# The feed-forward of a hybrid decoder layer in parts of 6, 14, 12 and 12 gated blocks, where it was 8, 16, 8 and 12

## The chip, the cores and the metric

The kernel runs on one core of a Trainium2 chip. The metric is the device time of one launch in microseconds. Before the change three runs took 1701.47, 1701.69 and 1701.87 us; the median is 1701.69.

## What is computed

One layer of a decoder trunk, for a prompt of 256 positions and a sample group of 8 × 4 positions that share the weights; 288 positions in all, model width 2048, feed-forward width 5632. Cut to what matters here:

```
z  = x @ w_in                        -> h, Bg, Cg, q, k, v, g_a, g_b
x1 = LN1(ALPHA*x + (sigmoid(g_a)*(A @ w_a) + sigmoid(g_b)*(B @ w_b)) @ w_out)
a, b = split(x1 @ w_up, 2)           # 5632 columns each
a    = causal width-3 depthwise convolution of a
y  = LN2(ALPHA*x1 + (silu(a) * b) @ w_down)
```

A is a gated short convolution and B an attention over dilated windows. The caches and convolution states that go with them are returned too.

## The kernel before

All activations lie transposed: 128 features on the partitions, the 288 positions along the free dimension, stored as two halves of 144. A weight block is 128 output columns by all its input rows, loaded as 16 (or fewer) tiles of 128 × 128. Everything is float32; to multiply at full rate each operand is split into a rounded high part and the rest (`split`, L263: a cast on ACT, a subtraction on DVE), and a product adds three matmuls per tile: high × high (L257), low × high (L258), high × low (L259).

`product` (L237 and on) multiplies one block. It takes the weights that were split one call ago and has the next block loaded: `prepare` gets a buffer `wst` (three of them), has SP issue the load (L205), for every third or fourth block has SP issue a copy of a cache page from memory to memory (L161, `out_o_rest`), and splits the block into pairs `whi`/`wlo` of up to eight tiles each (four pairs). The result goes to one of five accumulators `acc`.

The feed-forward is the part from line 1202 on. Its 44 gated blocks are made in parts, whose sizes stand in `THIRDS`. In each part:

- for each gated block an up product for a (48 matmuls), then ACT brings it into `u`, the convolution runs on ACT and DVE (`cy`), a second up product for b, DVE gates (`ya`), and the split into `yah`/`yal` (ACT, DVE);
- then 16 down products, one for each block of 128 output features, each with 3 matmuls for each gated block of the part; DVE adds their result to the residual `dd` (L1259 in part 0, L1261 later).

The layout of `w_down` in memory follows the parts: a down block of part 0 is 8 tiles, 512 KB.

Part 0 differs. It starts before LN1's deviation is known: its up products multiply `x_gb`, the values ahead of the norm with two more columns (290 instead of 288), and `normed` (L1195 to L1198) applies mean and deviation to the result afterwards. Between the gated blocks of this part the residual `dd` itself is normed, a share of its 16 blocks after each gated block: POOL multiplies and adds (L1241, L1242), ACT scales (L1243). While part 0's down products run, `dd` is split into `xh`/`xl`, the input of the later parts. Part 1 also carries a step of the second norm's factors with each gated block.

The order of instructions on each engine is made by a scheduler when the kernel is built; it interleaves products where it expects a wait. Each engine then runs its list strictly in that order.

Of the kernel before, what the change touches and what calls it, by code (L numbers as in the profile page):

```python
# [30 lines left out]
FF = 5632  # L31
KF = FF // P
HK = KD // 2
THIRDS = (8, 16, 8, 12)
NG, NH = 3, 4
DIL = (1, 4, 16)
BAND = 128
# [70 lines left out]
def layer_kernel(ctx: ExitStack, tc: tile.TileContext, ins, outs):  # L108
# [14 lines left out]
    def sb(pl, shape, tag, dt=F32, bufs=None):  # L123
        return pl.tile(shape, dt, tag=tag, name=nm(tag), bufs=bufs)
# [49 lines left out]
    def weight_list():  # L174
# [8 lines left out]
        f = wd = 0  # L183
        for nf in THIRDS:
            for _ in range(2 * nf):
# [1023 lines left out]
    sums = []  # L1209
    for part, nf in enumerate(THIRDS):  # L1210
        gh = sb(big, [P, KD, T], "yah", F32R)
# [133 lines left out]
def _lay_out(i):  # L1345
# [17 lines left out]
    wd, k0 = [], 0  # L1363
    for nf in THIRDS:
        w = a["w_down"][k0 * P : (k0 + nf) * P].reshape(nf, P, KD, P)
# [98 lines left out]
```

## Time and profile before

| | |
|---|---|
| median of three runs | 1701.69 us |
| the profiled execution: time, span | 1701.91 us, 1700.1 us |
| part 0: up products, down products | 909.44 to 1004.16, 1004.16 to 1051.20 us |
| part 1 (16 blocks) | 1051.20 to 1333.44 us |
| part 2 (8 blocks) | 1333.44 to 1474.56 us |
| part 3 (12 blocks) and the last norm | from 1474.56 us |
| mean granted TensorE clock | 0.999 |

The span runs from the first to the last instruction of the core. The borders of the parts are the starts of their first matmuls. In a row of a timeline stand the start, the duration, the engine, the line, the operation, the tile written and those read, the shape and the count; in brackets how long the engine was idle ahead of it and what ended that.

### The profile page before, as it was taken

The page shows a single profiled execution, that of the slowest core. Times are in us where ns is not written, and L with a number is a line of the kernel's source. Part 1 is how long each engine was busy: PE and PEld are TensorE (multiplying, and loading weights), DVE is VectorE, ACT ScalarE, POOL GpSimd, SP SyncE. Part 2 cuts the span into 40 slices and gives each one's busy share as a digit, 9 for nine tenths or more (in the row PEclk, how much of TensorE's full clock was granted, in tenths as well). Part 3 has the DMA queues.
Part 4 walks back from the last instruction along what each step waited for, and adds up shares of the span by engine and source line. Part 5 has one row for each costly group of instructions (what it writes and reads, how often), then busy time and mean ns, then how long its engine had stood idle before and what let it go on. Part 6 is the DMA issues. An engine that isn't in the chain of part 4 may idle for free.

```text
span 1700.1 us, 34305 instructions
## 1 busy us (share of the span) xinstructions
PE 1692.8 (100%) x14094; PEld 1689.6 (99%) x14094; DVE 1197.0 (70%) x1548; ACT 943.0 (55%) x1684; POOL 398.3 (23%) x528
## 2 busy tenths in 40 slices
PE   9999999999999999999999999999999999999998
PEld 9999999999999999999999999999999999999998
DVE  5476779889887776655888886776554555555576
ACT  6477686665666655544546664555433454444455
POOL 0123242223332121111454440111100010011175
PEclk9999999999999999999999999999999999999999
DMA  8778777666678988577766658666666667766553
GB/s 314 273 295 350 285 282 312 245 251 245 248 290 313 333 308 335 214 261 255 280 237 223 226 214 322 225 257 225 230 238 225 223 227 249 293 223 250 200 175 112
DMA packets 61532, 436.16 MB, mean 257 GB/s; under 512 B 7936, under 2 KB 12032, under 8 KB 23680
## 3 DMA queue, kind: packets, MB, share of 16 engines
q1 hardware_dynamic: 60080, 430.15, 68.7%
q10 hardware_dynamic: 1296, 3.83, 0.6%
q8 instruction: 110, 1.80, 0.4%
q14 instruction: 46, 0.38, 0.1%
HBM read 427.50 MB, written 94.53 MB: 307 GB/s over the span
## 4 chain that ended last, share of the span: by engine, by line
PE 99%; ACT 0%; DMA 0%; SPq 0%; DVE 0%; ACTq 0%; issue 0%
PE acc L257 32%; PE acc L258 32%; PE acc L259 32%; PE acc L342 1%; ACT yah L1148 0%; DMA yah<-in_x 0%; PE acc L443 0%; PE att L490 0%; PE acc L490 0%; SPq L297 0%; ACT xh L309 0%; PE acc L1129 0%; PE acc L1125 0%; PE long L490 0%; PE acc L1126 0%; ACT yal L309 0%
## 5 line engine op out<-in xcount | busy, mean ns | idle before, releaser
L263 DVE TENSOR_TENSOR wlo<-wst,whi 128x1024 fp32r<-128x1024 f32 (+1 forms) x579 | 743.9, 1287 | 392.5 <-ACT whi L263 390.1
L263 ACT CAST whi<-wst 128x1024 fp32r<-128x1024 f32 (+1 forms) x579 | 588.6, 1019 | 652.8 <-PE acc L258 588.8
L257 PE MATMUL acc<-xh,whi 128*128 128x288 f32 (+1 forms) x3216 | 920.3, 286 | 0.0
L258 PE MATMUL acc<-xl,whi 128*128 128x288 f32 (+1 forms) x3216 | 920.0, 286 | 0.0
L259 PE MATMUL acc<-xh,wlo 128*128 128x288 f32 (+1 forms) x3216 | 920.0, 286 | 0.0
L257 PEld LDWEIGHTS acc<-xh,whi 128*128 128x128 f32 x3216 | 607.8, 189 | 0.5 <-issue 0.4
L258 PEld LDWEIGHTS acc<-xl,whi 128*128 128x128 f32 x3216 | 607.8, 189 | 0.0
L259 PEld LDWEIGHTS acc<-xh,wlo 128*128 128x128 f32 x3216 | 607.8, 189 | 0.0
L258 PE MATMUL acc<-yal,whi 128*128 128x288 f32 x1216 | 347.5, 286 | 0.0
L259 PE MATMUL acc<-yah,wlo 128*128 128x288 f32 x1216 | 347.4, 286 | 0.0
L257 PE MATMUL acc<-yah,whi 128*128 128x288 f32 x1216 | 347.2, 286 | 0.0
L258 PEld LDWEIGHTS acc<-yal,whi 128*128 128x128 f32 x1216 | 229.8, 189 | 0.0
L259 PEld LDWEIGHTS acc<-yah,wlo 128*128 128x128 f32 x1216 | 229.7, 189 | 0.0
L257 PEld LDWEIGHTS acc<-yah,whi 128*128 128x128 f32 x1216 | 229.6, 189 | 0.0
L909 POOL COPY qk_s<-u 128x2 f32<-128x2 f32 x44 | 37.0, 842 | 535.7 <-ACT u L1223 487.3
L897 DVE SCALAR_TENSOR_TENSOR cy<-u,prm,cy 128x304 f32<-128x304 f32 x120 | 72.4, 603 | 7.0 <-ACT cy L895 4.3
L613 POOL TENSOR_TENSOR cache<-cache,cst 128x1024 f32<-128x1024 f32 x16 | 34.8, 2181 | 109.4 <-DMA cache<-in_cv 57.0
L613 POOL TENSOR_TENSOR cache<-cache,qk_s 128x1024 f32<-128x1024 f32 x16 | 33.3, 2084 | 64.8 <-DMA cache<-in_ck 64.5
L920 DVE TENSOR_TENSOR ya<-cy,acc 128x256 f32<-128x256 f32 x104 | 27.6, 308 | 26.6 <-PE acc L259 26.2
L263 ACT CAST yah<-ya 128x288 fp32r<-128x288 f32 x76 | 32.6, 428 | 23.8 <-DVE ya L920 14.6
L611 ACT ACTIVATE cache<-cache,qk_s 128x128 f32<-128x128 f32 x128 | 40.5, 392 | 0.0
L611 ACT ACTIVATE cache<-cache,cst 128x128 f32<-128x128 f32 x128 | 40.0, 390 | 0.0
(281 smaller groups left out, 1185.4 us busy)
## 6 DMA issues: line engine op xcount, KB each, us to landing
wst<-in_w_in SPq DMA_DIRECT2D x112, 1024.0 KB, 5.4
wst<-in_w_up SPq DMA_DIRECT2D x88, 1024.0 KB, 4.9
cache<-in_ck SPq DMA_DIRECT2D x18, 1024.0 KB, 7.8
cache<-in_cv SPq DMA_DIRECT2D x18, 1024.0 KB, 8.2
wst<-in_w_a SPq DMA_DIRECT2D x16, 1024.0 KB, 6.5
wst<-in_w_out SPq DMA_DIRECT2D x16, 1024.0 KB, 5.1
wst<-in_w_down SPq DMA_DIRECT2D x32, 512.0 KB, 4.7
wst<-in_w_down SPq DMA_DIRECT2D x16, 1024.0 KB, 4.9
```

The lines of the kernel that those rows point to most:

```text
L257: pe.matmul(out, hi[:, c, :], xh_k, start=k == 0, stop=False)
L258: pe.matmul(out, hi[:, c, :], xl_k, start=False, stop=False)
L259: last_mm[0] = pe.matmul(out, lo[:, c, :], xh_k, start=False, stop=k == nk - 1)
L263: return act.copy(hi, src), dve.tensor_tensor(lo, src, f32(hi), ALU.subtract)
L342: i = pe.matmul(o[b], first_w(term == 2, b, k), xk, start=k == 0 and term == 0, stop=k == KD - 1 and term == 2,)
L611: behind(act.activation(o[:, a, b], t[:, a, b], AF.Copy, scale=w[:, a, b : b + 1]), w_split[0])
L613: behind(pool.tensor_tensor(o, t, w.unsqueeze(3).broadcast_to([P, *n]), ALU.mult), w_split[1])
L897: dve.scalar_tensor_tensor(y, u[:, i : i + YW], prm[:, w0 + i : w0 + i + 1], y, ALU.mult, ALU.add)
L909: pool.tensor_copy(dst[:, 0:2], u[:, SEQ : SEQ + 2])
L920: dve.tensor_tensor(a, b, c, ALU.mult)
```

## The change

One line:

```
-THIRDS = (8, 16, 8, 12)
+THIRDS = (6, 14, 12, 12)
```

Part 0 has six gated blocks, so 12 up products of 290 columns instead of 16, and the four that leave are multiplied with the normed input at 288 columns in later parts. Its down blocks are six tiles (384 KB). Part 1 has 14 blocks (down blocks split as 8 + 6 tiles), part 2 has 12 (8 + 4). The numbers of up products, down products and matmuls stay. `w_down` is laid out accordingly ahead of the launch.

The share of residual blocks that part 0 norms after its gated block k is `range(k * KD // nf, (k + 1) * KD // nf)` with KD = 16: two after each of eight, and 2, 3, 3, 2, 3, 3 after six.

On POOL, at the last gated block of part 0, before (`u_12323` is that block's input of the convolution, `u_13167` one of the next part's):

```order
L909 COPY qk_s_11189<-u_12323 128x2
L910 COPY qk_s_11189<-u_12323 128x16
L1241 TENSOR_TENSOR dd_10040<-dd_10040,cache_10041 128x288 x2
L1242 TENSOR_TENSOR dd_10040<-dd_10040,cache_10041 128x288 x2
L888 MEMSET u_13167 128x2
```

and now:

```order
L909 COPY qk_s_11189<-u_12027 128x2
L910 COPY qk_s_11189<-u_12027 128x16
L1241 TENSOR_TENSOR dd_10040<-dd_10040,cache_10041 128x288 x3
L1242 TENSOR_TENSOR dd_10040<-dd_10040,cache_10041 128x288 x3
L888 MEMSET u_12778 128x2
```

Each of the two lines runs three times instead of twice. On ACT at the same place, before:

```order
L263 CAST whi_12483<-wst_12481 128x1024
L1195 COPY wgb_12396<-acc_12346 128x2
L1226 ACTIVATE cy_12335<-cy_12335 128x304
L1243 ACTIVATE dd_10040<-dd_10040,prm_179 128x288 x2
L263 CAST yah_11193<-ya_12395 128x288
L263 CAST xh_86<-dd_10040 128x2x144 x3
L263 CAST whi_12517<-wst_12515 128x1024
```

and now:

```order
L263 CAST whi_12178<-wst_12175 128x768
L1195 COPY wgb_12100<-acc_12050 128x2
L1226 ACTIVATE cy_12039<-cy_12039 128x304
L1243 ACTIVATE dd_10040<-dd_10040,prm_179 128x288 x3
L263 CAST yah_11193<-ya_12099 128x288
L263 CAST xh_86<-dd_10040 128x2x144 x3
L263 CAST whi_12206<-wst_12204 128x768
```

The cast of the last gated block, `yah`, stands behind three L1243 instead of two; the weight block behind it is that of down product 4 (counted from 0) in both.

On TensorE, where the first down products of part 0 come to their last gated block; before, `acc_12418`, `acc_12453` and `acc_12487` are down products 0, 1 and 2, and 57 matmuls of them have run:

```order
L259 MATMUL acc_12487<-yah_11193,wlo_12450 128x288
L257 MATMUL acc_12418<-yah_11193,whi_12342 128x288
L257 MATMUL acc_12453<-yah_11193,whi_12414 128x288
L257 MATMUL acc_12487<-yah_11193,whi_12449 128x288
L258 MATMUL acc_12487<-yal_11194,whi_12449 128x288
L258 MATMUL acc_12418<-yal_11194,whi_12342 128x288
```

Now `acc_12125`, `acc_12153`, `acc_12182` and `acc_12210` are down products 0 to 3, and 53 matmuls of them (15, 15, 15 and 8) have run:

```order
L258 MATMUL acc_12210<-yal_11194,whi_12178 128x288
L257 MATMUL acc_12125<-yah_11193,whi_12046 128x288
L257 MATMUL acc_12153<-yah_11193,whi_12121 128x288
L257 MATMUL acc_12182<-yah_11193,whi_12149 128x288
L259 MATMUL acc_12210<-yah_11193,wlo_12179 128x288
L258 MATMUL acc_12125<-yal_11194,whi_12046 128x288
```

Nineteen matmuls on come down products 4 and 5 (`acc_12238`, `acc_12267`), the first two matmuls of each ahead of the first that reads `wlo_12207`:

```order
L259 MATMUL acc_12210<-yah_11193,wlo_12179 128x288
L257 MATMUL acc_12238<-yah_11193,whi_12206 128x288
L258 MATMUL acc_12238<-yal_11194,whi_12206 128x288
L257 MATMUL acc_12267<-yah_11193,whi_12234 128x288
L258 MATMUL acc_12267<-yal_11194,whi_12234 128x288
L259 MATMUL acc_12238<-yah_11193,wlo_12207 128x288
```

So four products are interleaved instead of three, and the fourth doesn't run whole behind them. On DVE behind the last gated block, before:

```order
L263 TENSOR_TENSOR yal_11194<-ya_12395,yah_11193 128x288
L263 TENSOR_TENSOR xl_87<-dd_10040,xh_86 128x2x144 x3
L1259 SCALAR_TENSOR_TENSOR dd_10040<-dd_10040,acc_12418 128x288
L1259 SCALAR_TENSOR_TENSOR dd_10040<-dd_10040,acc_12453 128x288
L263 TENSOR_TENSOR wlo_12518<-wst_12515,whi_12517 128x1024
```

and now:

```order
L263 TENSOR_TENSOR yal_11194<-ya_12099,yah_11193 128x288
L263 TENSOR_TENSOR xl_87<-dd_10040,xh_86 128x2x144 x3
L1259 SCALAR_TENSOR_TENSOR dd_10040<-dd_10040,acc_12125 128x288
L1259 SCALAR_TENSOR_TENSOR dd_10040<-dd_10040,acc_12153 128x288
L1259 SCALAR_TENSOR_TENSOR dd_10040<-dd_10040,acc_12182 128x288
L263 TENSOR_TENSOR wlo_12207<-wst_12204,whi_12206 128x768
```

The rest of down product 4's weights, `wlo`, comes behind three additions to the residual instead of two.

## The prediction

> **What bounds the kernel now.** I read the head of the page, then the chain that ended last, then what TensorE waited for, then the feed-forward's stretches.
>
> ```profile
> span 1700.1 us, 34305 instructions
> PE 1692.8 (100%) x14094; PEld 1689.6 (99%) x14094; DVE 1197.0 (70%) x1548; ACT 943.0 (55%) x1684; POOL 398.3 (23%) x528
> PE 99%; ACT 0%; DMA 0%; SPq 0%; DVE 0%; ACTq 0%; issue 0%
> PE acc L342 <- ACT yal L309: 1.1, 1, 1.1
> PE acc L273 <- PEq L1451: 0.8, 1, 0.8
> ```
>
> TensorE (PE) is the chain. Its only two waits, 1.9 us together, are in the first ten microseconds. So nothing that is made faster on another engine can help, and the change can do two things: alter TensorE's own work, or open a wait where there is none.
>
> ```profile
> 909.44 0.29 PE L257 MATMUL acc<-xh,whi 128*128 128x290 f32 x1
> 1004.16 0.29 PE L257 MATMUL acc<-yah,whi 128*128 128x288 f32 x1
> 1051.20 0.29 PE L257 MATMUL acc<-xh,whi 128*128 128x288 f32 x1
> 1239.36 0.29 PE L257 MATMUL acc<-yah,whi 128*128 128x288 f32 x1
> 1004.16:1051.20 47.04, 47.04 (x386) 47.04 (x385) 34.57 (x55) 23.86 (x37) 4.74 (x6) 1.00 0.82 299
> ```
>
> These are the first matmuls of part 0's 16 up products, of its 16 down products, of part 1's 32 up products and of its down products, and the stretch of part 0's down products (busy PE, PEld, DVE, ACT, POOL; clock; DMA share; GB/s). I call the moment 1004.16, where part 0's up products end, U.
>
> **TensorE's own work: −0.16 us.** An up product is 48 matmuls. Part 0's have 290 columns and take (1004.16 − 909.44) / 768 = 0.1233 us each; part 1's have 288 and take (1239.36 − 1051.20) / 1536 = 0.1225 us. Four products leave part 0: 4 × 48 × 0.0008 = 0.16 us. All other matmuls stay, at 0.1225 us. The gain is certain and under a tenth of what a measurement can tell here (0.2%, 3.4 us).
>
> **The wait for the last gated block.** Down product 0 needs all blocks of `yah`/`yal`, the last one made after U. The scheduler covers that by running the first blocks of several down products: 21 + 21 + 15 = 57 matmuls before, 15 + 15 + 15 + 8 = 53 now, so the last block is wanted at U + 6.98 before and at U + 53 × 0.1225 = U + 6.49 now. When it came:
>
> ```profile
> 1003.72 2.12 POOL L1241 TENSOR_TENSOR dd<-dd,cache 128x288 f32<-128x288 f32 x2
> 1005.80 2.75 POOL L1242 TENSOR_TENSOR dd<-dd,cache 128x288 f32<-128x288 f32 x2
> 1007.62 0.63 ACT L1243 ACTIVATE dd<-dd,prm 128x288 f32<-128x288 f32 x1 [1.69 <-POOL dd L1242]
> 1008.59 0.63 ACT L1243 ACTIVATE dd<-dd,prm 128x288 f32<-128x288 f32 x1 [0.34 <-POOL dd L1242]
> 1009.18 0.43 ACT L263 CAST yah<-ya 128x288 fp32r<-128x288 f32 x1
> 1009.51 1.09 ACT L263 CAST xh<-dd 128x288 fp32r<-128x288 f32 x3
> 1011.15 0.53 PE L257 MATMUL acc<-yah,whi 128*128 128x288 f32 x3
> L1242 POOL TENSOR_TENSOR dd<-dd,cache 128x288 f32<-128x288 f32 x16 | 21.3, 1351 | 0.0
> L1241 POOL TENSOR_TENSOR dd<-dd,cache 128x288 f32<-128x288 f32 x16 | 15.0, 955 | 0.0
> ```
>
> The cast `yah` stands on ACT behind the rows L1243, and these wait for POOL. It ended at 1009.61, U + 5.45; the matmul that reads it started at 1011.15: 1.5 us to spare. With six gated blocks 16 residual blocks fall 2, 3, 3, 2, 3, 3 on them instead of two on each, so the last one carries three: one more L1241 and one more L1242, at the mean of their rows 0.955 + 1.351 = 2.31 us. POOL then ends at 1008.55 + 2.31 = 1010.86. The block ahead has three as well, its `yah` and the work behind it come later on ACT and DVE, and I add 0.15 us (0 to 0.8) for POOL's later start. L1243 follows 0.04 later and lasts 0.63, the cast ends 0.39 after it: 1010.86 + 0.15 + 0.04 + 0.63 + 0.39 = 1012.07, U + 7.91. TensorE waits 7.91 − 6.49 = **1.4 us**. At the least, with two POOL operations of 0.95, it is 1.0; with the late start and a further L1242 slowed as the first of this pair was (1.8 against 1.0), 2.6.
>
> **The second wait: weights of down product 4.** Only four pairs of `whi`/`wlo` exist, and products 0 to 3, interleaved, hold all of them. Before, three were interleaved and the fourth ran whole after them, which hid the next split. Y is the end of the cast `yah`.
>
> ```profile
> 1009.64 0.46 DVE L263 TENSOR_TENSOR yal<-ya,yah 128x288 fp32r<-128x288 f32 x1 [0.50 <-ACT yah L263]
> 1010.01 1.19 DVE L263 TENSOR_TENSOR xl<-dd,xh 128x288 fp32r<-128x288 f32 x3
> 1012.08 0.82 DVE L1259 SCALAR_TENSOR_TENSOR dd<-dd,acc 128x288 f32<-128x288 f32 x2 [0.88 <-PE acc L259]
> 1013.04 1.23 DVE L263 TENSOR_TENSOR wlo<-wst,whi 128x1024 fp32r<-128x1024 f32 x1
> L263 DVE TENSOR_TENSOR wlo<-wst,whi 128x512 fp32r<-128x512 f32 x34 | 25.6, 753 | 21.6 <-ACT whi L263 21.5
> L263 ACT CAST whi<-wst 128x512 fp32r<-128x512 f32 x34 | 21.0, 617 | 37.9 <-PE acc L258 36.6 <-DMA wst<-in_w_in 1.3
> ```
>
> DVE now has `yal`, three `xl`, three L1259 (two before) and then `wlo`. By these rows `yal` and `xl` end at Y + 1.60, the three L1259, 0.37 apart, at Y + 2.7, and a `wlo` of 768 columns, between 0.75 and 1.23, takes 0.99: Y + 3.6. TensorE, which goes on at Y + 0.03, has 23 matmuls until it wants it, Y + 2.85. That is **0.75 us** (0.3 if `wlo` takes its shortest row and the chain starts early, 0.9 with the longest).
>
> **The later down products: weights at a faster beat.** A down product of part 0 takes 18 × 0.1225 = 2.2 us instead of 2.94. Three load buffers `wst` make a loop: `wlo` frees one, SP issues, the block lands, ACT casts, DVE subtracts; it must close within three products, 6.6 us now, 8.8 before.
>
> ```profile
> wst<-in_w_down SPq DMA_DIRECT2D x10, 512.0 KB, 4.9
> out_o_rest<-in_rest SPq DMA_DIRECT2D x5, 7.5
> DMA to landing us min/median/max: 3.8/4.9/7.2
> 1018.23 1.05 ACT L263 CAST whi<-wst 128x1024 fp32r<-128x1024 f32 x1 [2.33 <-DMA wst<-in_w_down]
> ```
>
> 512 KB land in 3.8 to 7.2 us, 4.9 in the median, and the copies `out_o_rest` share the engines. For 384 KB I take 4.6 (3.5 to 5.5). The cast is 0.83 (between 0.62 and 1.05), the subtraction 0.99, and 0.1 goes between them: 6.5 us. That just closes. It doesn't behind a copy: the stretch moves 299 GB/s × 47.04 us / 16 = 0.88 MB a product, 0.52 of it weights; now 0.75 MB in 2.2 us, 339 GB/s, a DMA share of 0.82 × 339 / 299 = 0.93. I put down 0.8 us for two or three late blocks, the first up product behind them included, whose 1 MB has the same loop; bounds 0 and 3.
>
> The Trainium skill, "DMA: Bandwidth & Descriptors", section Bandwidth, asks to batch transfers to 1 MiB or more, which speaks against shrinking these from 512 to 384 KB; its section Anatomy of one DMA has a fit (for the other DMA path) of 2.0 us plus the bytes at 436 GB/s, by which 384 KB would take an estimated 2.9 us, the loop would close in 4.8 and the 0.8 would go from the sum. The trace has 4.9 for 512 KB where the fit gives 3.2, so the rows stand.
>
> Elsewhere I cost the change at nothing. The later boundaries have covers of 13 × 3 = 39 and 33 matmuls (4.8 and 4.0 us); part 3 has 33 already and shows no wait. Sixteen more weight splits (part 1's blocks are 8 + 6, part 2's 8 + 4) go to stretches where DVE and ACT have room: DVE was busy 34.57 of 47.04 us in the fullest, part 0's own, which loses none. Were that cover gone they would cost 16 × 0.75 us.
>
> **The sum** is −0.16 + 1.4 + 0.75 + 0.8 = +2.8 us. The profiled execution took 1701.91, 0.22 over the median, so against the median 1701.69 + 2.8 = **1704.5 us**, +0.16%: within 0.2%, though not zero.
>
> **Rivals.** *Supply runs dry (0.32).* The loop takes 7.5 us because landings grow to 5.6 at a DMA share of 0.93: 0.9 us late for each three products, four rounds after product 4, less about 1 us in hand: 2.6 in place of 0.8, and with POOL's chain at its upper bound 1.2 more: 1704.5 + 3.0 = 1707.5, slower by 0.34%. It decides from a mean landing of about 4.7 us on. For it: 4.9 now. Against: fewer bytes, and each wait of TensorE gives the loop time.
>
> *The waits do not come (0.08).* The gated chain ends early enough, say because POOL is less disturbed and the three L1243 run while DVE still makes `ya`: only the gain and some tenths are left, 1701.5 to 1702.3. Against it: ACT already waited for POOL at this place, 1.69 and 0.34 us, and two more operations stand there.
>
> *The clock drops (0.02).* TensorE paced slower at the kernel's start:
>
> ```profile
> L273 PE MATMUL acc<-const-float32-0.0 128*128 128x288 f32 x16 | 3.9, 431 | 0.8 <-PEq L1451 0.8
> 8.39 15.70 PE acc L342 x126
> ```
>
> Sixteen matmuls took 3.9 us, 0.24 each. If a wait set that off again for as long, it would cost 16 × (0.24 − 0.1225) = 1.9 us: 1706.4. But after the 1.1 us wait ahead of 8.39, 126 matmuls ran at 15.70 / 126 = 0.125. The Trainium skill, "TensorE: Matmul & The Clock Gate", section What's actually happening, has the clock halve after an idle window of some 3.4 us; no wait I expect is that long.
>
> **How the numbers follow.** The forecast has 0.58 and spans +1.1 us (all terms at their least) to +3.4, where the supply case takes over: 1702.8 to 1705.1. The range reaches through the supply case and takes in the upper edge of the no-wait case: 1702.3 to 1707.6. Slower by over 0.2% (above 1705.1) is that rival, the clock and the upper edge of the forecast: 0.38. Faster by over 0.2% would need 3.4 us of TensorE work gone, and 0.16 goes: 0.02. The rest, 0.60, is within 0.2%.
>
> **What would show it.** In the new profile TensorE's waits should have a row on ACT `yah` at L257 of 1 to 2.6 us near 988 (U is 23.7 us earlier, at 980.5); a second one of 0.3 to 0.9 on DVE `wlo` at L259 some 3 us on; and small ones on `whi` or `wlo` in the next 35 us. Part 0's down stretch should be 35.3 us plus these. ACT's L1243 there should come in threes, with POOL as releaser. No wait for `yah` would make the first term wrong; waits of over 2 us after the third down product would make the supply rival right; waits elsewhere would mean that I missed a place.

## The result and the profile after

The changed kernel takes 1707.12 us (median of six runs, 1706.35 to 1709.09) against 1701.73 for the kernel before (six runs, 1701.47 to 1702.01): ratio 1.0034, 95% interval 1.0023 to 1.0044. It is 0.3% slower. The profiled execution is the lowest of the six, 1706.35 us. In experiment 1 one execution of five took 3372.47 us at a granted clock of 0.84, and the ratio given there is that of the other four.

The head of its page with the engines' shares of the chain that ended last, and then the view of all that TensorE (PE) waited for (us in total, times, longest):

```profile
span 1704.5 us, 34334 instructions
PE 1694.9 (99%) x14094; PEld 1690.2 (99%) x14094; DVE 1195.5 (70%) x1554; ACT 944.3 (55%) x1696; POOL 394.0 (23%) x528
PE 92%; DVE 2%; POOL 2%; ACT 2%; DMA 1%; issue 1%; SPq 0%; ACTq 0%; DVEq 0%
```

```profile
PE acc L259 <- DVE wlo L263: 1.5, 4, 0.5
PE acc L257 <- ACT yah L263: 1.3, 1, 1.3
PE acc L273 <- PEq L1451: 0.8, 1, 0.8
PE acc L257 <- ACT whi L263: 0.5, 1, 0.5
```

The chain was TensorE alone (99%); now 7% of it runs over VectorE (DVE), GpSimd (POOL), ScalarE (ACT) and the DMAs. The rows on `wlo`, `yah` and `whi` are new. They all lie in part 0's down products and the first up product of part 1, as TensorE's timeline shows:

```profile
979.93 0.29 PE L257 MATMUL acc<-yah,whi 128*128 128x288 f32 x1
...
987.90 0.64 PE L257 MATMUL acc<-yah,whi 128*128 128x288 f32 x3 [1.32 <-ACT yah L263]
...
990.78 0.39 PE L257 MATMUL acc<-yah,whi 128*128 128x288 f32 x1
991.00 0.29 PE L258 MATMUL acc<-yal,whi 128*128 128x288 f32 x1
...
991.46 0.39 PE L259 MATMUL acc<-yah,wlo 128*128 128x288 f32 x1 [0.17 <-DVE wlo L263]
...
1004.18 0.29 PE L259 MATMUL acc<-yah,wlo 128*128 128x288 f32 x1
1004.93 0.39 PE L257 MATMUL acc<-yah,whi 128*128 128x288 f32 x1 [0.46 <-ACT whi L263]
1005.15 0.29 PE L258 MATMUL acc<-yal,whi 128*128 128x288 f32 x1
...
1005.92 0.39 PE L259 MATMUL acc<-yah,wlo 128*128 128x288 f32 x1 [0.48 <-DVE wlo L263]
...
1015.34 0.39 PE L259 MATMUL acc<-yah,wlo 128*128 128x288 f32 x1 [0.33 <-DVE wlo L263]
...
1019.61 0.29 PE L257 MATMUL acc<-xh,whi 128*128 128x288 f32 x1
...
1020.51 0.39 PE L259 MATMUL acc<-xh,wlo 128*128 128x288 f32 x1 [0.50 <-DVE wlo L263]
```

Count start to start. Two undisturbed matmuls are 0.1225 us apart; 1004.18 to 1004.93 are 0.75, so 0.63 were lost. The bracket says 0.46, because it counts from the end of a matmul and these overlap. The matmul after a wait comes 0.23 later, not 0.12 (1004.93 to 1005.15), so each wait costs another 0.10. Summed over all gaps in the trace, these included:

| place | lost, us |
|---|---|
| the last gated block, near 987.9 | 1.59 |
| weights of down products 4 and 5, near 991 | 0.74 |
| supply: product 10 (1.47), product 14 (0.60), first up product of part 1 (0.76) | 2.83 |
| all | 5.16 |

Part 0's down stretch (979.93 to 1019.61) is 39.7 us where 288 matmuls of 0.1225 are 35.3. From the first up product of part 0 (908.89; 909.44 before) to the last matmul the profile after has 789.73 us, the one before 784.74: 4.99 us more, which is 5.16 less the 0.16 of TensorE's own work. The end moved by 0.55 less than that, since this execution reached the feed-forward earlier: the 1.1 us wait for `yal` at L342, at the start of the kernel before, is not in its view, and the matmul that stood behind it starts at 7.84 instead of 8.39. The medians are 5.4 apart.

The weights, at product 10. The issues of SP, then the casts of ScalarE (ACT) in the same stretch:

```profile
994.28 0.33 SPq L205 DMA_DIRECT2D wst<-in_w_down  x1
994.66 0.52 SPq L161 DMA_DIRECT2D out_o_rest<-in_rest  x1
996.44 9.78 SPq L205 DMA_DIRECT2D wst<-in_w_down  x4
```

```profile
998.42 0.83 ACT L263 CAST whi<-wst 128x768 fp32r<-128x768 f32 x1 [0.72 <-DVE wlo L263]
...
1004.04 0.83 ACT L263 CAST whi<-wst 128x768 fp32r<-128x768 f32 x1 [4.45 <-DMA wst<-in_w_down]
...
1005.12 0.83 ACT L263 CAST whi<-wst 128x768 fp32r<-128x768 f32 x1
```

A cache copy stands at 994.66, the load behind it (the first of the four in the last row) is issued at 996.44, and the cast that needs it starts at 1004.04: 7.6 us later, after 4.45 us with nothing to cast. By the DMAs' completions, all 384 KB loads issued from 976 us on fall into two groups: behind a copy, that is with over 2 us of a copy still to land when the load is issued, they take 5.6 to 7.5 us; the others land in 3.0 to 4.1. The median says nothing of this; it was 4.9 us for 512 KB and is, in the view of the DMAs from 978 to 1020 us (issues, KB each, median us to landing):

```profile
wst<-in_w_down SPq DMA_DIRECT2D x12, 384.0 KB, 4.8
```

### The profile page after: what moved, and what is told of

Its sections match the earlier page's. It is cut to its first block, busy times and chain, and to the rows that moved or that the text cites. A ratio compares the mean times of both kernels' runs of the same rounds, so it can differ in the third digit from the quotient of the medians.

```text
span 1704.5 us, 34334 instructions
## 1 busy us (share of the span) xinstructions
PE 1694.9 (99%) x14094; PEld 1690.2 (99%) x14094; DVE 1195.5 (70%) x1554; ACT 944.3 (55%) x1696; POOL 394.0 (23%) x528
## 4 chain that ended last, share of the span: by engine, by line
PE 92%; DVE 2%; POOL 2%; ACT 2%; DMA 1%; issue 1%; SPq 0%; ACTq 0%; DVEq 0%
PE acc L257 30%; PE acc L259 30%; PE acc L258 30%; DVE wlo L263 1%; PE acc L342 1%; DMA wst<-in_w_down 1%; POOL dd L1242 1%; ACT whi L263 1%; POOL dd L1241 1%; DMA wst<-in_w_up 0%; ACT yah L1148 0%; PE acc L443 0%; DMA yah<-in_x 0%; ACT dd L1243 0%; ACT u L1220 0%
## 5 line engine op out<-in xcount | busy, mean ns | idle before, releaser
L263 DVE TENSOR_TENSOR wlo<-wst,whi 128x1024 fp32r<-128x1024 f32 (+2 forms) x595 | 749.2, 1261 | 423.3 <-ACT whi L263 421.3
L263 ACT CAST whi<-wst 128x1024 fp32r<-128x1024 f32 (+2 forms) x595 | 591.4, 997 | 649.6 <-PE acc L258 580.5
L897 DVE SCALAR_TENSOR_TENSOR cy<-u,prm,cy 128x304 f32<-128x304 f32 x120 | 70.8, 590 | 7.8 <-ACT cy L895 5.5
L263 ACT CAST yah<-ya 128x288 fp32r<-128x288 f32 x76 | 32.5, 428 | 23.2 <-DVE ya L920 14.5
```

The costliest lines, as they stand in the source:

```text
L263: return act.copy(hi, src), dve.tensor_tensor(lo, src, f32(hi), ALU.subtract)
L897: dve.scalar_tensor_tensor(y, u[:, i : i + YW], prm[:, w0 + i : w0 + i + 1], y, ALU.mult, ALU.add)
```

## The experiments

Each ran beside the kernel before (1701.44 to 1701.52 in these comparisons). "Lag" is how long after TensorE's last matmul of a gated block's up products the cast `yah` of that block ends, worked out from the trace; for the last block that is the time after U. Lines of code that an edit adds move the numbers behind them by one to four, so L263 may be L264 or L265.

**1. Residual blocks given out otherwise.** Part 0's shares become 3, 3, 3, 3, 2, 2 instead of 2, 3, 3, 2, 3, 3.

```
+SHARES = (0, 3, 6, 9, 12, 14, 16)
-                for i in range(k * KD // nf, (k + 1) * KD // nf):
+                for i in range(SHARES[k], SHARES[k + 1]):
```

> Part 0's six gated blocks as in the changed kernel, but the first norm's residual blocks are given out so that only two, and not three, stand ahead of the last two gated blocks' casts; nothing is computed differently. My theory (the wait for the last gated block comes from the third residual block on ScalarE, 1.6 us with its restart): that wait goes or falls under 0.3 us, the 0.74 us wait for the weights of down product 4 shrinks, the small supply waits stay; 1.6 to 2.2 us less than the changed kernel, about 1705.1. Rival (the six blocks are themselves too short a cover, whatever the residual's place): the wait stays over 1 us and the time within 0.5 us of the changed kernel. Rival (supply alone decides): the wait goes and the supply waits grow by as much.

Measured: 1707.29 us, ratio 1.0035 (1.0021 to 1.0048). A miss: nothing gained. The wait for `yah` is still 1.3 us, a new one of 1.1 us opened on `wlo` just ahead of it, and all gaps together are 5.8 us.

**2. No copies behind part 0's down loads.**

```
-        if n >= 20 and n % 10 in (0, 3, 7):
+        if n >= 20 and n % 10 in (0, 3, 7) and not 174 <= n <= 190:
```

> The five cache copies that stand among part 0's down loads are moved to other loads later in the program; all copies are still made. My theory (the supply waits, 2.84 us, come when a 384 KB load lands behind a copy, 5.6 to 7.5 us instead of 3.0 to 4.0): the waits at down products 5, 10 and 14 and at the first up product after go, those for the last gated block and for product 4 stay (1.6 and 0.74 us); 2 to 2.9 us less than the changed kernel, about 1704.5, and the runs lie closer together than its 2.7 us. Rival (three buffers are too few for blocks of 2.2 us, copies or not): the supply waits stay, and the time falls by under 0.5 us.

Measured: 1703.75 us, ratio 1.0013 (1.0005 to 1.0022), eleven runs within 0.9 us. That is 0.75 us below the 1704.5 that I expected. The waits at products 10 and 14 and at the up product behind them are gone, 2.36 us of gaps are left, and these are `yah` and products 4 and 5 as in the changed kernel. The small wait on `whi` of product 5, which I had put with the supply, stayed: it belongs to the second wait. The casts of the same stretch, ScalarE's timeline:

```profile
998.94 0.83 ACT L263 CAST whi<-wst 128x768 fp32r<-128x768 f32 x1 [0.69 <-DVE wlo L263]
...
1000.96 0.83 ACT L263 CAST whi<-wst 128x768 fp32r<-128x768 f32 x1 [0.85 <-PE acc L258]
...
1002.92 0.83 ACT L263 CAST whi<-wst 128x768 fp32r<-128x768 f32 x1 [0.79 <-PE acc L258]
```

They now wait for TensorE to free a weight pair: the supply is ahead. So the three-buffer loop does close with a product every 2.2 us, as long as no copy stands in it.

**3. Both edits.**

> Both edits together, the residual's shares and the copies moved. My theory (two causes that add up): all waits of part 0's down stretch gone but for some tenths, 4 to 5 us less than the changed kernel, 1701.6 to 1702.4, the kernel before within 0.05%. Rival (three buffers too few, or the shorter cover): 1704 or more.

Measured: 1705.10 us, ratio 1.0022 (1.0012 to 1.0031): 1.35 us worse than without the new shares. My theory of the first wait fell here. With two residual blocks ahead of it, the last `yah` came later than with three, at U + 8.98 instead of U + 7.95, and a new wait opened on `wlo` at 987 (1.1 us). The timelines of ScalarE and VectorE (DVE):

```profile
985.29 0.63 ACT L1244 ACTIVATE dd<-dd,prm 128x288 f32<-128x288 f32 x1 [1.04 <-POOL dd L1243]
985.82 0.44 ACT L1227 ACTIVATE cy<-cy 128x304 f32<-128x304 f32 x1
986.28 0.63 ACT L1244 ACTIVATE dd<-dd,prm 128x288 f32<-128x288 f32 x1
988.90 0.43 ACT L264 CAST yah<-ya 128x288 fp32r<-128x288 f32 x1 [1.99 <-DVE ya L926]
```

```profile
985.51 1.55 DVE L264 TENSOR_TENSOR wlo<-wst,whi 128x768 fp32r<-128x768 f32 x1
986.99 0.45 DVE L1198 TENSOR_TENSOR h<-acc,cache 128x288 f32<-128x288 f32 x1
987.47 0.52 DVE L1199 SCALAR_TENSOR_TENSOR h<-cache,wgb,h 128x288 f32<-128x288 f32 x1
988.09 0.48 DVE L923 SCALAR_TENSOR_TENSOR ya<-h,wgb,cy 128x256 f32<-128x256 f32 x1
988.49 0.38 DVE L926 SCALAR_TENSOR_TENSOR ya<-h,wgb,cy 128x16 f32<-128x16 f32 x2
```

ScalarE was done with its residual work at 986.9 and then idle for 1.99 us. What came late was `ya` from VectorE, and VectorE was late from the beats ahead. That gave a new theory, of the beat, the time from one gated block to the next on the vector engines (VectorE, GpSimd and ScalarE together). TensorE takes 11.84 us for the two up products of a gated block. In the traces a gated block with three residual blocks follows the one ahead of it by 12.34 us in steady state, one with two by less than 11.84 where there is something to catch up:

| kernel | residual blocks with each gated block | lag of each block, us |
|---|---|---|
| before | 2 2 2 2 2 2 2 2 | 8.96 6.82 6.04 6.33 6.00 6.00 6.00 5.44 |
| changed | 2 3 3 2 3 3 | 8.96 8.31 8.81 7.81 8.32 7.92 |
| both edits | 3 3 3 3 2 2 | 10.06 9.79 10.28 10.78 9.58 8.98 |

**4. Two residual blocks with each of six, the last four later.** No copies behind part 0's down loads either.

```
+SHARES = (0, 2, 4, 6, 8, 10, 12)
+LATE = {1: 12, 3: 13, 5: 14, 7: 15}
...
+                if i in LATE:
+                    j = LATE[i]
+                    with tc.issue_after(i_dd.ins):
+                        dve.tensor_tensor(dd[:, j], dd[:, j], n1.r, ALU.mult)
+                        dve.tensor_tensor(dd[:, j], dd[:, j], n1.nmr, ALU.add)
+                    act.activation(dd[:, j], dd[:, j], AF.Identity, bias=n1.at(n1.b, j), scale=n1.at(n1.g, j))
```

> No copies behind part 0's down loads, and only two residual blocks with each of the six gated blocks; the last four are made during the first down products, their multiply and add on VectorE. New theory, from the runs with other shares (the beat counts, not the place: a gated block with three residual blocks takes the vector engines 12.34 us against TensorE's 11.84, one with two keeps up, so six beats with 16 residual blocks end about 8 us after TensorE's last up product and ones with 12 end 5.5 to 6 us after it): the 1.6 us wait for the last gated block goes, though two residual blocks still stand right ahead of its cast, as in the run with both edits, where it stayed; 1701.3 to 1702.4. Rival (six blocks are too short a cover in any case): the wait stays over 1 us and the time at 1703.5 or more.

Measured: 1702.59 us, ratio 1.0006 (0.9997 to 1.0015), 0.2 us over what I expected. The wait for `yah` is gone, the last lag is 5.53. Two residual blocks stand ahead of the last cast as in experiment 3, so their place isn't what decides. The second wait stayed at 0.7 us; two of the late instructions on VectorE stand ahead of the weights of products 4 and 5, and with these three products later (experiment 10) it was 0.3.

**5. The same work without GpSimd's part.** As experiment 2, with POOL's two instructions for each residual block left out; ScalarE keeps its three activations ahead of the last cast.

```
-                    with tc.issue_after(i_rows.ins):
-                        pool.tensor_tensor(dd[:, i], dd[:, i], n1.r, ALU.mult)
-                        pool.tensor_tensor(dd[:, i], dd[:, i], n1.nmr, ALU.add)
-                    act.activation(...)
+                    with tc.issue_after(i_silu.ins):
+                        act.activation(...)
```

> As the run without copies behind part 0's down loads (1703.75), but GpSimd's two instructions of each residual block, the multiply and the add, are left out: the residual of the first norm isn't computed rightly. ScalarE's activation of each block stays, three ahead of the last gated block's cast. Theory of the beat (GpSimd's work makes VectorE's instructions beside it longer, the 128x768 weight rest 1.55 us instead of 0.95, and so the beat): the last gated block at most 5.5 us after the last up product, no wait for it, 1701.3 to 1702.0. Rival (three activations in ScalarE's list are enough to make it late): the cast stays over 6.5 us after, with a wait.

Measured: 1701.69 us, ratio 1.0000 (0.9991 to 1.0010), last lag 4.18, no wait for `yah`. ScalarE and VectorE near the last gated block:

```profile
981.51 1.65 ACT L1241 ACTIVATE dd<-dd,prm 128x288 f32<-128x288 f32 x3
984.03 0.43 ACT L263 CAST yah<-ya 128x288 fp32r<-128x288 f32 x1 [0.87 <-DVE ya L925]
```

```profile
979.65 1.10 DVE L897 SCALAR_TENSOR_TENSOR cy<-u,prm,cy 128x304 f32<-128x304 f32 x2
981.23 0.96 DVE L263 TENSOR_TENSOR wlo<-wst,whi 128x768 fp32r<-128x768 f32 x1 [0.47 <-ACT whi L263]
```

Three activations are in the list as in the changed kernel and cost nothing. VectorE's instructions are short without GpSimd beside them: here two L897 take 1.10 us and the `wlo` behind them 0.96, in the changed kernel, with POOL's L1241 and L1242 running, 2.05 and 1.55. So GpSimd's work is what makes the beat too long. How it does so this experiment leaves open, because it takes out two things at once: GpSimd and VectorE slowing each other, and ScalarE's waits for GpSimd. For the first the pair 0.96 and 1.55 speaks. The Trainium skill, "SBUF — State Buffer", section Who interferes with whom, says that a VectorE tensor-tensor with both inputs in SBUF contends with GpSimd's reads, because its second input comes through a read interface that the two share; that pair agrees with it. The second stands in the changed kernel's own trace, in the beat of its third gated block, one of 12.34 us (timelines of POOL, ScalarE and VectorE):

```profile
945.28 2.77 POOL L1241 TENSOR_TENSOR dd<-dd,cache 128x288 f32<-128x288 f32 x3
948.02 2.75 POOL L1242 TENSOR_TENSOR dd<-dd,cache 128x288 f32<-128x288 f32 x2
951.07 0.81 POOL L1242 TENSOR_TENSOR dd<-dd,cache 128x288 f32<-128x288 f32 x1
950.80 0.63 ACT L1243 ACTIVATE dd<-dd,prm 128x288 f32<-128x288 f32 x1 [0.35 <-POOL dd L1242]
951.34 1.03 ACT L263 CAST whi<-wst 128x1024 fp32r<-128x1024 f32 x1
952.40 1.23 DVE L263 TENSOR_TENSOR wlo<-wst,whi 128x1024 fp32r<-128x1024 f32 x1 [0.49 <-ACT whi L263]
```

ScalarE's cast of the next weights stands behind an L1243 that waits for POOL, and VectorE, done with `ya` half a microsecond before, waits for that cast. VectorE's next `h` stands behind this `wlo`, ScalarE's next `u` needs that `h`, and POOL's next work starts with that `u`. So this beat is a loop over three engines, and in the part of it that is shown here POOL and ScalarE set the time, not VectorE's slowed instructions beside them. POOL is slowed too: its first five operations take 5.5 us, where the last one takes 0.81. Five at 0.81 would take an estimated 4.05, 1.5 us less, which is more than the 0.5 by which this beat exceeds TensorE's. So the wait in ScalarE's queue and the slowing probably act together; no run takes out one without the other.

**6. Six staging buffers.** The changed kernel, all copies in place; `wst` as six buffers of eight tiles in the same memory.

```
-        st = sb(wp, [P, KD, P], "wst")
+            st = sb(wp, [P, HK, P], "wst", bufs=6)
```

> The changed kernel with its copies where they are, but the weight staging split into six buffers of eight tiles in the same memory (a block of 16 tiles comes as two loads); part 0's six-tile down blocks so have six buffers and not three. Theory (the copies delay a load to 5.6 to 7.5 us, and three buffers of 2.2 us each, 6.6 us, can't cover that, six can): the supply waits go as they did without the copies, 1703.4 to 1704.4. Rival (the copies take bandwidth or their place in the queue, and the depth of the buffers doesn't matter): 1706 or more.

Measured: 1703.85 us, ratio 1.0014 (1.0005 to 1.0022), as without the copies. The landing of the loads did not get better; the profile's view of the tile `wst` over this stretch has, for the changed kernel and then for this one:

```profile
DMA to landing us min/median/max: 3.1/5.6/9.0
```

```profile
DMA to landing us min/median/max: 3.0/5.6/7.8
```

These two views mix the down loads with up blocks, 1 MB in one and 512 KB in the other; the 384 KB loads behind a copy took 5.6 to 7.5 us with three buffers and 6.2 to 7.0 with six. But what ScalarE's casts wait for there (us in total, times, longest) was, in the changed kernel, a DMA, and is TensorE's release of a weight pair with six buffers:

```profile
ACT whi L263 <- DMA wst<-in_w_down: 12.6, 5, 4.5
```

```profile
ACT whi L265 <- PE acc L260: 13.5, 13, 1.9
```

No cast waits for a DMA there any more, and TensorE's waits are those of experiment 2. So a late landing needs a short loop to hurt: the copies and the three buffers cause the supply waits together, and either mends them.

**7. Parts of 7, 13, 12 and 12.**

> Parts of 7, 13, 12 and 12 blocks, nothing else. New theory of the beat: residual blocks 2, 2, 2, 3, 2, 2 and 3 over seven beats, so the vector engines are back by the end; the last gated block 6.5 to 7.0 us after the last up product against a cover of 57 matmuls, 7.0 us: no wait or up to 0.3 us. Supply: a beat of 2.57 us makes three buffers 7.7 us, over most landings behind a copy: 0 to 1.5 us. 1701.5 to 1703.3. Rival of the first theory (three residual blocks right ahead of the last cast cost about 1 us): 1702.7 to 1704.5, with a wait for it.

Measured: 1702.09 us, ratio 1.0003 (0.9994 to 1.0012). The last block carries three residual blocks, its lag is 6.77, and there is no wait for it. What is left, 1.24 us of gaps at 1012 to 1014, is a supply wait: the load for it was issued right behind a copy and landed after 7.9 us.

**8. The kernel before with three residual blocks at the end** (2, 2, 2, 2, 2, 2, 1, 3).

> The kernel before, parts of 8, 16, 8 and 12, with the residual blocks given out as 2, 2, 2, 2, 2, 2, 1 and 3, so that three stand ahead of the last gated block's cast. Theory of the prediction (the third residual block in ScalarE's list is the cause): last gated block about 7.9 us after the last up product, against a cover of 58 matmuls, 7.1 us: a wait of about 0.8 us, 1702.2 to 1702.6. New theory of the beat (eight beats carry 16, the engines are not behind): 6.5 to 7.0 us, no wait, 1701.3 to 1701.9.

Measured: 1701.68 us, ratio 1.0001 (0.9992 to 1.0010). The last lag is 7.12 against 5.44, so the third block does cost time where it stands, about 1.7 us; but the cover of 58 matmuls takes all but 0.2 us. I had expected 6.5 to 7.0.

**9. Parts of 8, 12, 12 and 12**: part 0 as before, the rest as changed or nearly so.

> Parts of 8, 12, 12 and 12 blocks: part 0 as in the kernel before, the rest changed. My theory (the change costs only in part 0's stretch): the time of the kernel before within 0.5 us, 1701.3 to 1702.2. Rival (the later parts of other sizes, with their other up and down blocks, carry some of the cost): 1 us or more above it.

Measured: 1701.67 us, ratio 1.0001 (0.9992 to 1.0010), and no gap in the feed-forward. Later parts of other sizes cost nothing.

**10. Both causes mended in the changed kernel**: six buffers with all copies in place, and the late residual of experiment 4 three products later (`LATE = {4: 12, 6: 13, 8: 14, 10: 15}`).

> All copies where the changed kernel has them, six staging buffers of eight tiles, two residual blocks with each gated block and the last four during down products 4 to 10 on VectorE. Both causes are mended: no wait for the last gated block, no supply waits, the wait at down product 4 gone or under 0.3 us; 1701.2 to 1702.0, so the kernel before less 0.16 us at the best, and no difference that can be measured. Rival (a rest of about 1 us stays in the change whatever is mended, as in the late-residual run's 1702.59): 1702.3 or more.

Measured: 1701.56 us, ratio 0.9999 (0.9990 to 1.0008). Part 0's down stretch, the windows view of this run:

```profile
980.31:1015.92 35.61, 35.58 (x291) 35.37 (x290) 33.73 (x63) 23.33 (x41) 3.26 (x5) 1.00 0.84 293
```

The stretch is 35.61 us, 0.3 above its matmuls, at a clock of 1.00. From the first up product to the last matmul this run has 784.89 us; less the 0.33 of its gaps that is 0.18 below the kernel before. That is the whole gain that parts of 6, 14, 12 and 12 hold, and no version tried here beats the kernel before by more than a measurement can tell.

## Why the prediction was right or wrong

The range held the time (1707.12 in 1702.3 to 1707.6), the forecast did not: 1704.5 with a span of its own to 1705.1, and "within 0.2%" had the largest chance, where the kernel is slower by 0.32%. The supply rival, at 1707.5, came nearest.

- **TensorE's own work, −0.16 us.** Right: −0.17 (4.99 − 5.16), and −0.18 in experiment 10.
- **The wait for the last gated block, 1.4 us.** The place, the time (U + 7.91 forecast, U + 7.92 measured) and the cost (1.59, of which 0.10 is the slow restart) were right, the composition was not, so that the time came out to 0.01 us was luck. I gave the third residual block 2.31 us and the delay from the block ahead 0.15. With three behind two full beats of two (experiment 7, the nearest run, its down blocks one tile longer) the lag is 6.77, so the third block is worth 1.3 over before's 5.44, and the other 1.15 (7.92 − 6.77) come from the beats ahead, which had three as well. By experiment 8, where the block ahead carries only one, it is 1.7 and 0.8. Either way the beats ahead give several times the 0.15. At 6.77 the wait would be 0.3 us by the changed kernel's cover of 6.49. I read the end of the chain in one place, POOL and ScalarE's queue, where in truth VectorE arrives at the same moment, as the timelines of the changed kernel show:

```profile
985.87 0.63 ACT L1243 ACTIVATE dd<-dd,prm 128x288 f32<-128x288 f32 x1 [0.85 <-POOL dd L1242]
986.84 0.63 ACT L1243 ACTIVATE dd<-dd,prm 128x288 f32<-128x288 f32 x1 [0.34 <-POOL dd L1242]
987.42 0.43 ACT L263 CAST yah<-ya 128x288 fp32r<-128x288 f32 x1
```

```profile
983.63 1.55 DVE L263 TENSOR_TENSOR wlo<-wst,whi 128x768 fp32r<-128x768 f32 x1
...
987.01 0.38 DVE L925 SCALAR_TENSOR_TENSOR ya<-h,wgb,cy 128x16 f32<-128x16 f32 x2
```

  Two L925, from 987.01 on and 0.38 together, leave `ya` ready at 987.39, and the cast starts at 987.42, when ScalarE's last L1243 is done too. Two paths end together, so shortening one alone (experiment 1) could not help, and the releaser in the brackets names only one of them. (The upper bound of this term, 2.6, has the 0.15 in it twice; by its own rows it is 2.5. Nothing hangs on that.)
- **The second wait, 0.75 us.** Right, 0.74.
- **The supply, 0.8 us.** This is the term that was mis-sized: 2.83, at the upper bound of 3. The step "two or three late blocks" had the count right (three places) and the price wrong. It set the whole stretch at one landing of 4.6 us, closed the loop at 6.5 against 6.6, and added tenths for copies. The landings are two groups: 3.0 to 4.1 us, with which the loop closes easily (experiment 2), and 5.6 to 7.5 behind a copy, where it takes about 7.5 to 9.4 (with the cast's 0.83, the subtraction's 0.95 and 0.1). One such block is up to 2.8 us late; what TensorE has in hand takes off the rest.
- **The fit that I set aside**, because 512 KB took 4.9 us where it gives 3.2. The Trainium skill's estimate for 384 KB, 2.9 us ("DMA: Bandwidth & Descriptors", section Anatomy of one DMA), agrees with the loads of the changed kernel that land alone (3.0). By that fit the term would have been 0, and with the copies it was 2.83. The median that I held against it belongs to loads that are not alone: in the kernel before, the load issued at 1014.29, with nothing ahead of it, took 3.84, and the next two, with loads but no copy ahead (one was issued 0.4 us behind the second), 4.91 and 4.83. The Trainium skill's section Queues, rings and completion order, on the same page, says that on each DMA engine the descriptors of an issuing engine's ring are consumed in ring order. The 5.6 to 7.5 us of a load behind a copy agree with it, but it gives no price for that.
- **The supply rival, 2.6 us and 1707.5.** Its size was right and its trigger partly: it wanted all landings to grow with the DMA share to 5.6 and every third product to be late. The share of the stretch fell instead, as these windows of the changed kernel show (0.74 in the column ahead of the GB/s; 0.82 before), and the loads without a copy ahead were quick.

```profile
979.93:1019.61 39.68, 36.89 (x291) 35.60 (x289) 29.00 (x52) 20.55 (x38) 7.20 (x10) 1.00 0.74 263
```

  Its other half, POOL's chain at the upper bound, did not come.
- **The clock rival** did not come: 1.00 in that row, and after each wait the step is back to 0.12 us with the second matmul.
- **Elsewhere nothing.** Right: behind the places of the table the profile after has no gap that the profile before lacks, and experiment 9 agrees.

What stays open: the medians of the changed kernel and the kernel before are 5.4 us apart, the gaps of the profiled run explain 5.0. That run is the fastest of its six. The missing 0.4 is probably supply as well. The runs with supply waits scatter more (2.7 us, and 2.5 in experiment 7, against 0.9 to 1.5 in experiments 2, 4, 6 and 10). And where the supply waits are gone, in experiments 2 and 6, the median is 2.2 and 2.3 us above that of the kernel before, so 3.1 to 3.2 went from the 5.4, where the profiled run has 2.83 of these waits. No second profile of the changed kernel shows it. How a beat with three residual blocks divides into the engines' slowing of each other and ScalarE's wait for POOL stays open too.

## What to carry to other kernels

When the same side work is spread over fewer steps, follow one whole step in steady state through all the vector engines' queues, with their waits for each other and at the durations that they have side by side, and compare its length with TensorE's. A lag that grows by half a microsecond a step is not seen at the last step alone, and moving work to an earlier step doesn't remove it. For a ring of load buffers, look at the distribution of landings and at what is queued ahead of each load, not at the median: shrinking the blocks shortens the cover of every load, the late ones too. Here the short blocks needed more buffers, or no copy ahead of them; the DMA engines were 0.74 busy. Buffers can be cut finer in the same memory.

## What the runs showed of the hardware

- In these traces a matmul that waited for a semaphore is followed by one that starts 0.23 us later instead of 0.12; the next is back to 0.12. So a wait costs 0.10 us over its own length, which for short waits (0.2 us) is half as much again.
- VectorE's 128x768 subtraction took 0.96 us alone and 1.55 beside GpSimd's tensor-tensor on 128x288, and that tensor-tensor took 0.81 at its shortest and 1.4 in the mean of the two L1242 of 2.75 us.
- A 384 KB load issued by SP landed in 3.0 to 4.1 us, and in 5.6 to 7.5 when a memory-to-memory copy issued ahead of it had over 2 us still to run.
- With the staging cut into half-size buffers and loads, the kernel did as well or better: two loads of 512 KB for a 1 MB block brought no wait, although the landings in part 0's down stretch were no faster.
